# Moving the elementwise work of a two-layer hybrid network's fronts from GpSimd to VectorE

## The chip, the cores and the metric

The kernel runs on one core of a Trainium2 chip. What is measured is the time of one execution on the device, in microseconds (us). A core has five engines that work at the same time, each through its own queue and in the order of that queue: TensorE (PE in the rows; PEld is its weight load), VectorE (DVE), ScalarE (ACT), GpSimd (POOL) and SyncE (SP), which here only issues DMAs. Engines wait for one another by semaphores.

## The reference

Two layers of a diffusion backbone over 256 latent tokens and 256 context tokens, width 1024, float32. A layer is, cut to what matters:

```
h      = modulate(rmsnorm(x), shift, scale)
ua, ub, uatt, us5, ug = split(h @ w_in)
y      = rwkv7(ua), gla(ub), window_attention(uatt), s5(us5)     # 4 mixers, width 256
merged = sum over i of sigmoid(ug_i) * (y_i @ w_branch[i])       # 4 gates, width 1024
x      = x + mod * (merged @ w_out)
tokens = modulate(rmsnorm(x), ...)
x      = x + mod * hierarchical_moe(tokens)    # top group of 4, top 2 of its 8 experts
```

RWKV-7 and S5 scan the tokens in both directions, GLA works in chunks of 64 tokens, attention has a window of 128, a sink and the context as keys. In the last layer the context tokens are only an input of the mixers, so there merges and MoE have 256 columns and not 512.

## The kernel before

**Stages.** A layer is a *front* (projection, mixers, gates, output projection, router) and a *MoE*. In the profiled execution the front of layer 0 ends at about 890 us, its MoE at about 1440 us, the front of layer 1 at about 2130 us, and the MoE of layer 1 ends the program. In a front, the first stretch (0 to 200 us, and 1440 to 1660 us) holds the S5 tables, S5's four groups of channels in both directions and GLA; then come RWKV's projection and attention; then RWKV's "units" (330 to 600 us, and 1780 to 1990 us), small chains of 64x64 matmuls and DVE operations, between which the matmuls of gate merges are woven; then the last merges and the tail.

**Weights in two parts.** Front matmuls take float32 weights as a rounded part and a remainder. `gsplit` (L237) loads 128x1024 weights into `g`, lets ACT copy them into a rounded tile `h`, and takes the remainder `r = g - h`; both tiles are called `gs` in the rows. `proj` (L255) multiplies by `h` first, 16 matmuls, and by `r` last, 8 matmuls. Tile `r` has two places in most stretches and one in the units and merges of layer 0 (L1852), so a subtraction can start when PE has let go of the `r` before the last, or of the last. There are 53 such pairs in each front.

**Who does the elementwise work.** The helpers `act`, `tt`, `stt` and `mm` (L270 to L286) issue nearly everything, so most rows carry their lines; `tt` goes to DVE unless it is given another engine. Before, GpSimd has: the remainders; the token shift sums `us` of RWKV (L338); one of four key products `bk` of each RWKV unit (L493, the other three are on DVE); the end-of-chunk key product `ke` of GLA (L749) and half of the copies of its state, `sb` (L798); two of the six rope operations per token tile (L860, L863); of the S5 quarters one of each two products (`t<-fq,tb`, L1197, L1200, L1214); the remainder `hl` of half of the modulated activations (L1330); the sum of merges in `acc` (L1397); the second half of the residual `x` (L1410); and the split of every second token tile for the MoE (L1436). It also sets tiles to constants (memset), and in the MoE it adds expert results.

**Order.** The program is written as a list of operations; a scheduler then puts each engine's instructions in an order of its own by a plan, so that one engine's queue mixes instructions of several mixers. At run time no instruction passes another of its queue.

Of the kernel before, what the change touches and what calls it, by code (L numbers as in the profile page):

```python
# [175 lines left out]
class Net:  # L176
# [60 lines left out]
    def gsplit(self, src):  # L237

        w = self.gload(src)
        k, n = src.shape[1:]  # L240
        i = self.gi % 2
        self.gi += 1
        h, r = (p.tile([128, 1024], F32R, tag=t, name="gs")[:, 0:k * n].rearrange("p (k n) -> p k n", k=k)
                for p, t in (self.gp[i], self.gp[2 + i]))
        self.act(h, w, AF.Copy)
        self.tt(r, w, h.bitcast(F32), OP.subtract, self.nc.gpsimd)
        return h, r

    def mm3(self, out, a, b, start, stop):
# [44 lines left out]
    def rwkv_in(self, l, h, lo, pool, tp, between):  # L294
# [29 lines left out]
        for sec in (3, 1, 0, 2):  # L324
            for hf in range(2):
                a, n = (lo, nlo) if sec == 0 else (0, 512)
                ns = n // 256
                ps = self.pa()
                self.proj(ps[:, 0:n], io["w_in_rwkv"][l, 2 * sec + hf], h, a)
                between()  # L330
                ci = sec * 2 + hf
                u = tp.tile([128, 2, 258], F32, tag="upad", name="u")
                G.memset(u[:, :, 0:258:257], 0.0)
                psv = ps[:, 0:n].rearrange("p (s t) -> p s t", t=256)
                self.act(u[:, 0:ns, 1:257], psv, AF.Copy)
                s = tp.tile([128, 512], F32, tag="us", name="us")
                sv = s[:, 0:n].rearrange("p (s t) -> p s t", t=256)
                self.tt(sv, u[:, 0:ns, 0:256], u[:, 0:ns, 2:258], OP.add, G)  # L338
                dst = xa[:, hf, :] if sec == 3 else r[:, hf, :] if sec == 0 else kv[:, sec - 1, hf, :]
                self.act(dst, ps[:, 0:n], AF.Copy, scale=omu[:, ci:ci + 1])  # L340
                self.stt(dst, s[:, 0:n], hmu[:, ci:ci + 1], dst, OP.mult, OP.add)
# [68 lines left out]
    def rwkv_finish(self, l, hf, st, y, pool):  # L410

        prm = self.prm[l]
        r, k_, v, lo = st["r"], st["k"], st["v"], st["lo"]
        blk = self.cst[:, C_BLK:C_BLK + 128]
        nlo = 512 - lo
        ps = self.pc()
        self.mm(ps[:, 0:nlo], blk, y, True, True)
        yc = pool.tile([128, nlo], F32, tag="yc", name="yc")
        self.stt(yc, ps[:, 0:nlo], -1.0 / 64, y, OP.mult, OP.add)
        s2 = st["pool"].tile([128, 512], F32, tag="pi", name="s2")[:, 0:nlo]  # L420
        self.act(s2, yc, AF.Square)
        ps = self.pc()
        self.mm(ps[:, 0:nlo], blk, s2, True, True)
        self.rsq(s2, ps[:, 0:nlo], 1.0 / 64, 1)
        self.stt(yc, yc, prm[:, P_LNG + hf:P_LNG + hf + 1], s2, OP.mult, OP.mult)
        self.stt(s2, r[:, hf, :], prm[:, P_RK + hf:P_RK + hf + 1], k_[:, hf, lo:512], OP.mult, OP.mult)
        ps = self.pc()
        self.mm(ps[:, 0:nlo], blk, s2, True, True)
        self.tt(s2, ps[:, 0:nlo], v[:, hf, lo:512], OP.mult)
        self.tt(yc, yc, s2, OP.add, self.nc.gpsimd)  # L430
        ps = self.pc()
        self.mm(ps[:, 0:nlo], st["g2"][:, hf * 128:hf * 128 + 128], st["sg"], True, True)
        self.tt(y, ps[:, 0:nlo], yc, OP.mult)
# [30 lines left out]
    def rwkv_sub(self, hf, d, s, u, S0, st, na, y, pool):  # L464
# [16 lines left out]
        n = st["n"]  # L481
# [8 lines left out]
        for f in range(2):  # L490
            fv = fo[f][:, ts].rearrange("p (j t) -> p j t", t=64)
            self.tt(bk[E[f], :, f, :], ch(na[:, ts])[E[f]], fv[E[f]], OP.mult)
            self.tt(bk[E[1 - f], :, f, :], ch(k_[:, hf, ts])[E[1 - f]], fv[E[1 - f]], OP.mult, V if f else G)  # L493

        sm = st["p0"].tile([128, 4, 2, 192], F32, tag="sm", bufs=st["depth"], name="sm")
        for jp in range(2):
# [235 lines left out]
    def gla_dir(self, d, la, q, kx, v, mg, oT, lo, pool):  # L732
# [13 lines left out]
        ke = pool.tile([128, 512], F32, tag="ke", name="ke")  # L746
        self.tt(ke.rearrange("p (c t) -> p c t", t=64), tot.to_broadcast([128, 8, 64]), c3, OP.subtract)
        self.act(ke, ke, AF.Exp, scale=1.0 / 16)
        self.tt(ke, ke, kx, OP.mult, G)  # L749
        qd = pool.tile([128, 512], F32, tag="qd", name="qd")  # L750
        self.act(qd[:, lo:512], cum[:, lo:512], AF.Exp, scale=1.0 / 16)
        self.tt(qd[:, lo:512], qd[:, lo:512], q[:, lo:512], OP.mult)
# [40 lines left out]
        for hp in range(2):  # L793
            for e in range(2):
                h = 2 * hp + e
                r = slice(32 * h, 32 * h + 32)
                for n, c in runs:
                    (G if e else V).tensor_copy(sb[r, c, e, :], S[r, n - 1, :])  # L798
                ps = self.pb()
                for c in range(c0, 8):  # L800
                    b, t = c % 2, c // 2
                    self.mm(ps[64 * b:64 * b + 64, 64 * t:64 * t + 64], ki[r, 64 * c:64 * c + 64],
                            qd[r, 64 * c:64 * c + 64], True, True)
                for b in range(2):
                    rb = slice(64 * b, 64 * b + 64)
                    self.tt(sc[rb, e, t0:4, b, :], ps[rb, 64 * t0:256].rearrange("p (t n) -> p t n", n=64),
                            mg[rb, None, :].to_broadcast([64, 4 - t0, 64]), OP.mult)
# [20 lines left out]
    def attn(self, l, h, yT, lo, pool):  # L828
# [23 lines left out]
        for t in range(2, 4):  # L852
# [4 lines left out]
            o = rot.rearrange("p (h z n) -> p h z n", h=6, z=2)  # L857
            tm = tm.rearrange("p (z h n) -> p z h n", z=2, h=6)
            self.tt(o[:, :, 0, :], raw[:, :, 0, :], cs, OP.mult)
            self.tt(tm[:, 0], raw[:, :, 1, :], sn, OP.mult, G)  # L860
            self.tt(o[:, :, 0, :], o[:, :, 0, :], tm[:, 0], OP.subtract)
            self.tt(o[:, :, 1, :], raw[:, :, 0, :], sn, OP.mult)
            self.tt(tm[:, 1], raw[:, :, 1, :], cs, OP.mult, G)  # L863
            self.tt(o[:, :, 1, :], o[:, :, 1, :], tm[:, 1], OP.add)
            qk[t] = rot
        qT = pool.tile([128, 2, 512], F32, name="qT")
# [253 lines left out]
    def s5_quarter(self, d, gb, lo, pr, tb, ug, ys, kd, t2, dd, pool):  # L1120
# [73 lines left out]
        zq = pool.tile([128, 2, 4, 64], F32, tag="zq", name="zq")  # L1194
        C, S_ = tb[:, 0, g4], tb[:, 1, g4]
        self.tt(s1[:, 0], fq[:, 0], C, OP.mult)
        self.tt(s1[:, 1], fq[:, 1], S_, OP.mult, G)  # L1197
        self.tt(zq[:, 0], s1[:, 0], s1[:, 1], OP.add)
        self.tt(s1[:, 0], fq[:, 1], C, OP.mult)
        self.tt(s1[:, 1], fq[:, 0], S_, OP.mult, G)  # L1200
        self.tt(zq[:, 1], s1[:, 0], s1[:, 1], OP.subtract)
        rh = pool.tile([128, 4, 64], F32, tag="rh", name="rh")
        self.tt(rh, self.mres[:, 0:256].rearrange("p (g n) -> p g n", g=4),
# [7 lines left out]
        for z in range(2):  # L1211
            a, b = (fq[:, 0], fq[:, 1]) if z == 0 else (fq[:, 1], fq[:, 0])
            self.tt(s1[:, 0], a, C, OP.mult)
            self.tt(s1[:, 1], b, S_, OP.mult, G)  # L1214
            op = OP.subtract if z == 0 else OP.add
            if d == 0:
                self.tt(xi[:, z, :, 1:64], s1[:, 0, :, 0:63], s1[:, 1, :, 0:63], op)
# [106 lines left out]
    def modulate(self, k, mc, h, src, tmp):  # L1324

        for s in range(2):
            t = slice(256 * s, 256 * s + 256)
            self.tsc(tmp[:, t], src[:, t], mc[:, 0, s, k:k + 1], OP.mult, mc[:, 1, s, k:k + 1], OP.add)
        self.act(h[0][:, k, :], tmp, AF.Copy)
        self.tt(h[1][:, k, :], tmp, h[0][:, k, :].bitcast(F32), OP.subtract, None if k % 2 else self.nc.gpsimd)  # L1330

    def rows(self, l, pool):

# [36 lines left out]
    def merge(self, l, i, h, yT, acc, lo, first, pool, between, pairs=None):  # L1370
# [5 lines left out]
        for c in range(8):  # L1376
# [17 lines left out]
                self.stt(o, sg, 1.0, pb, OP.add, OP.mult)  # L1394
            else:
                self.stt(sg, sg, 1.0, pb, OP.add, OP.mult)
                self.tt(o, o, sg, OP.add, nc.gpsimd)  # L1397

    def project(self, t, w, acc, x, bs, lo, pool):

# [2 lines left out]
        for n in range(2):  # L1403
# [3 lines left out]
            tm = pool.tile([128, 512], F32, tag="pm", bufs=2, name="pm")  # L1407
            self.tt(tm, ps, bs[s][:, 512 * n:512 * n + 512], OP.mult)
            xo = x[t][:, 512 * n:512 * n + 512]
            self.tt(xo, xo, tm, OP.add, self.nc.gpsimd if n else None)  # L1410


    def norm2(self, t, x, rw, lo, h2p, wr, lg, pool):
# [19 lines left out]
            (V.tensor_copy if kb else nc.scalar.copy)(hT[:, 4 * kb:4 * kb + 4, :].rearrange("p k n -> p (k n)"), ps)  # L1433
        for k in range(8):
            self.mm(lg[:, 36 * tl:36 * tl + 36], hT[:, k, :], wr[:, k, :], k == 0, k == 7)
        self.split3([h2p[:, i, tl, :] for i in range(3)], h2, G if t % 2 else V)  # L1436

    def split3(self, o, r, eng):

# [467 lines left out]
```

## Time and profile before

| | |
|---|---|
| three runs | 2632.54, 2640.57, 2654.95 us (median 2640.57) |
| profiled execution | 2633.36 us, of which the span is 2631.5 us |
| mean granted TensorE clock | 0.939 |
| busy: PE, DVE, ACT, POOL | 2392.9, 1167.7, 665.1, 705.6 us |
| front 0, MoE 0, front 1, MoE 1 (about) | 890, 550, 690, 500 us |

Busy times are sums over the span. "Idle before" counts the time in which an engine had nothing to run, and is put down to the work whose end came last. PEclk is the granted clock of TensorE in a stretch, where 1 is the higher of its two levels (2.4 GHz) and 0.5 the lower (1.2 GHz). A row `gs<-g,gs` is an instruction that writes a tile `gs` from tiles `g` and `gs`.

### The profile page before, as it was taken

What the parts mean: (1) busy time and instruction counts of PE and PEld (TensorE: products, weight loads), DVE (VectorE), ACT (ScalarE), POOL (GpSimd) and SP (SyncE); (2) the same over time, 40 slices, a digit from 0 to 9 for tenths busy, and PEclk for the clock granted to TensorE, in tenths of its full rate; (3) what the DMA queues carried; (4) which work ended last, traced back from release to release, by engine and by line L of the source; (5) the groups of instructions that cost most, each with busy time, mean ns of one, the idle gap of its engine ahead of it and who ended that gap; (6) DMA issues with size and microseconds to landing.
All of it is one profiled execution on the core that took longest, in us unless ns stands there. A gap on an engine that the chain in (4) does not pass through costs nothing. (4 is left out here: it accounts for less than half of the span.)

```text
span 2631.5 us, 42668 instructions
## 1 busy us (share of the span) xinstructions
PE 2392.9 (91%) x17303; PEld 1445.7 (55%) x17303; DVE 1167.7 (44%) x3013; ACT 665.1 (25%) x1187; POOL 705.6 (27%) x603
## 2 busy tenths in 40 slices
PE   5889989999999899999999788998989899999997
PEld 4666756666764544444443665776777544333332
DVE  6685467573224533122222678558373432222212
ACT  3243433322211211111111324432323211111111
POOL 2233411213521232232233334422224211111111
PEclk8988989999999899999999798778889989999999
DMA  6332111214542698888886243312224579999994
GB/s 222 107 122 89 60 42 36 69 37 171 191 168 87 276 389 352 320 326 316 351 317 271 94 157 127 105 47 64 60 75 166 220 312 419 411 394 403 390 405 166
DMA packets 143693, 548.24 MB, mean 208 GB/s; under 512 B 35028, under 2 KB 66132, under 8 KB 93060
## 3 DMA queue, kind: packets, MB, share of 16 engines
q1 hardware_dynamic: 138224, 539.51, 54.0%
q10 hardware_dynamic: 5268, 5.94, 0.7%
q8 instruction: 140, 2.29, 0.4%
q14 instruction: 61, 0.50, 0.1%
HBM read 541.78 MB, written 3.60 MB: 207 GB/s over the span
## 5 line engine op out<-in xcount | busy, mean ns | idle before, releaser
L270 PE MATMUL pa<-hh,gs 128*128 128x512 f32 (+2 forms) x1440 | 436.6, 378 | 12.0 <-ACT sg L273 4.3
L276 POOL TENSOR_TENSOR gs<-g,gs 128x1024 fp32r<-128x1024 f32 (+1 forms) x106 | 258.6, 2443 | 581.9 <-PE pa L270 231.2
L276 POOL TENSOR_TENSOR ta<-ta,mb 128x512 f32<-128x512 f32 x93 | 127.8, 1381 | 835.5 <-ACT ta L273 835.5
L270 PEld LDWEIGHTS pa<-hh,gs 128*128 128x128 f32 (+1 forms) x1440 | 265.2, 198 | 74.5 <-issue 18.3
L270 PE MATMUL pd<-w,hT 128*64 128x512 f32 x1024 | 276.6, 599 | 13.1 <-ACT hT L273 12.4
L270 PE MATMUL pa<-hl,gs 128*128 128x512 f32 (+2 forms) x720 | 263.2, 377 | 0.0
L270 PE MATMUL pgate<-w,xT 128*64 128x512 f32 x1024 | 251.3, 596 | 0.0
L270 PE MATMUL pup<-w,xT 128*64 128x512 f32 x1024 | 249.2, 594 | 0.0
L270 PEld LDWEIGHTS <-h2p 128*128 128x128 bf16 x2304 | 135.2, 100 | 78.0 <-issue 72.6
L270 PE MATMUL pg<-oh,h2p 128*128 128x128 bf16 x2304 | 163.5, 223 | 5.9 <-DVE nv L1686 4.2
L273 ACT ACTIVATE gs<-g 128x1024 fp32r<-128x1024 f32 (+1 forms) x106 | 110.4, 1044 | 221.9 <-PE pa L270 139.6
L270 PEld LDWEIGHTS pd<-w,hT 128*64 128x64 f32 x1024 | 81.5, 136 | 146.7 <-issue 124.6
L270 PEld LDWEIGHTS pa<-hl,gs 128*128 128x128 f32 (+1 forms) x720 | 144.6, 201 | 28.4 <-issue 9.4
L270 PEld LDWEIGHTS pup<-w,xT 128*64 128x64 f32 x1024 | 78.3, 137 | 143.2 <-issue 139.3
L270 PEld LDWEIGHTS pgate<-w,xT 128*64 128x64 f32 x1024 | 74.7, 137 | 139.6 <-issue 129.5
L270 PE MATMUL py<-yp,oT 128*128 128x512 f32 x384 | 132.3, 438 | 11.2 <-ACT ta L273 5.1
L286 DVE SCALAR_TENSOR_TENSOR hd<-hd,pgate 128x512 f32<-128x512 f32 x32 | 22.0, 688 | 246.4 <-ACT hd L273 246.3
L276 POOL TENSOR_TENSOR x<-x,ta 128x512 f32<-128x512 f32 x93 | 121.6, 1314 | 4.9
L270 PE MATMUL pa<-gs,hh 128*128 128x256 f32 x480 | 112.9, 330 | 7.3 <-POOL gs L276 6.9
L276 DVE TENSOR_TENSOR hd<-hd,pup 128x512 f32<-128x512 f32 x32 | 22.0, 688 | 217.9 <-PE pup L270 217.9
L286 DVE SCALAR_TENSOR_TENSOR yp<-pd,ws,yp 128x512 fp32r<-128x512 f32 x64 | 47.8, 747 | 152.6 <-ACT yp L273 152.6
L273 ACT ACTIVATE yp<-pd,ws 128x512 fp32r<-128x512 f32 x64 | 44.1, 688 | 272.9 <-PE pd L270 272.9
(505 smaller groups left out, 3692.1 us busy)
## 6 DMA issues: line engine op xcount, KB each, us to landing
w<-in_w_g SPq DMA_DIRECT2D x128, 1024.0 KB, 7.8
w<-in_w_d SPq DMA_DIRECT2D x128, 1024.0 KB, 10.3
w<-in_w_u SPq DMA_DIRECT2D x128, 1024.0 KB, 8.5
g<-in_w_ada SPq DMA_DIRECT2D x96, 512.0 KB, 3.7
g<-in_w_in_gate SPq DMA_DIRECT2D x64, 512.0 KB, 3.7
g<-in_w_in_rwkv SPq DMA_DIRECT2D x16, 512.0 KB, 3.6
wb<-in_w_branch SPq DMA_DIRECT2D x64, 128.0 KB, 2.9
w<-in_w_out SPq DMA_DIRECT2D x8, 1024.0 KB, 8.0
```

The source lines that it names most:

```text
L270: self.nc.tensor.matmul(out, lhsT, rhs, start=start, stop=stop, skip_group_check=True)
L273: self.nc.scalar.activation(out, in_, f, **kw)
L276: (eng or self.nc.vector).tensor_tensor(out, a, b, op)
L286: self.nc.vector.scalar_tensor_tensor(out, a, s, b, op0=op0, op1=op1)
```

## The change

Every `tt` of the list above loses its engine argument, or is given DVE, so that DVE runs it; the copies of GLA's state that GpSimd made are made by ACT. What is left to GpSimd in a front are memsets and copies of constants at the start. The MoE (`pair`) is as before. No tile, pool or loop is changed. The edits are all of one kind; the core of the diff:

```diff
@@ gsplit
         self.act(h, w, AF.Copy)
-        self.tt(r, w, h.bitcast(F32), OP.subtract, self.nc.gpsimd)
+        self.tt(r, w, h.bitcast(F32), OP.subtract)
@@ rwkv_in
-                self.tt(sv, u[:, 0:ns, 0:256], u[:, 0:ns, 2:258], OP.add, G)
+                self.tt(sv, u[:, 0:ns, 0:256], u[:, 0:ns, 2:258], OP.add)
@@ rwkv_finish
-        self.tt(yc, yc, s2, OP.add, self.nc.gpsimd)
+        self.tt(yc, yc, s2, OP.add)
@@ rwkv_sub
             self.tt(bk[E[f], :, f, :], ch(na[:, ts])[E[f]], fv[E[f]], OP.mult)
-            self.tt(bk[E[1 - f], :, f, :], ch(k_[:, hf, ts])[E[1 - f]], fv[E[1 - f]], OP.mult, V if f else G)
+            self.tt(bk[E[1 - f], :, f, :], ch(k_[:, hf, ts])[E[1 - f]], fv[E[1 - f]], OP.mult)
@@ gla_dir
-        self.tt(ke, ke, kx, OP.mult, G)
+        self.tt(ke, ke, kx, OP.mult)
...
-                    (G if e else V).tensor_copy(sb[r, c, e, :], S[r, n - 1, :])
+                    (nc.scalar.copy if e else V.tensor_copy)(sb[r, c, e, :], S[r, n - 1, :])
@@ attn (the same for tm[:, 1])
-            self.tt(tm[:, 0], raw[:, :, 1, :], sn, OP.mult, G)
+            self.tt(tm[:, 0], raw[:, :, 1, :], sn, OP.mult)
@@ s5_quarter (three lines of this kind)
-        self.tt(s1[:, 1], fq[:, 1], S_, OP.mult, G)
+        self.tt(s1[:, 1], fq[:, 1], S_, OP.mult)
@@ modulate
-        self.tt(h[1][:, k, :], tmp, h[0][:, k, :].bitcast(F32), OP.subtract, None if k % 2 else self.nc.gpsimd)
+        self.tt(h[1][:, k, :], tmp, h[0][:, k, :].bitcast(F32), OP.subtract)
@@ merge
-                self.tt(o, o, sg, OP.add, nc.gpsimd)
+                self.tt(o, o, sg, OP.add)
@@ project
-            self.tt(xo, xo, tm, OP.add, self.nc.gpsimd if n else None)
+            self.tt(xo, xo, tm, OP.add)
@@ norm2
-        self.split3([h2p[:, i, tl, :] for i in range(3)], h2, G if t % 2 else V)
+        self.split3([h2p[:, i, tl, :] for i in range(3)], h2, V)
```

The scheduler gives every engine a new order. On DVE, in the first stretch of layer 0, the power tables of S5 are made in a chain of small operations (`t` is a pair of products, `w` their sum or difference, `tb` the table). Before:

```order
L276 TENSOR_TENSOR t_474<-w_1077 128x8 x2
L276 TENSOR_TENSOR w_1090<-t_474 128x8
L276 TENSOR_TENSOR t_474<-w_1077 128x8 x2
L276 TENSOR_TENSOR w_1090<-t_474 128x8
L276 TENSOR_TENSOR t_474<-tb,w_1090 128x8x16 x2
```

With the change:

```order
L276 TENSOR_TENSOR t_474<-w_1077 128x8 x2
L276 TENSOR_TENSOR gs<-g,gs 128x1024
L276 TENSOR_TENSOR w_1090<-t_474 128x8
L286 SCALAR_TENSOR_TENSOR rg<-th__1933,pa 128x512
L276 TENSOR_TENSOR t_474<-w_1077 128x8 x2
L276 TENSOR_TENSOR w_1090<-t_474 128x8
L276 TENSOR_TENSOR t_474<-tb,w_1090 128x8x16 x2
```

A remainder now stands inside the chain, ahead of a 128x8 difference.

On DVE, in the RWKV units of layer 1, the key products `bk` of one unit stand between steps of a triangular inverse (`ti`, `tm`) of another. Before (the product `bk<-kv,sw` is on GpSimd):

```order
L276 TENSOR_TENSOR tm<-lt,ti 128x4x9
L276 TENSOR_TENSOR bk<-na,sw 64x4x64
L276 TENSOR_TENSOR ti<-ti,tm 128x4x9
L276 TENSOR_TENSOR ti<-ti,tm 128x4x14
L276 TENSOR_TENSOR tm<-lt,ti 128x4x8
L276 TENSOR_TENSOR bk<-na,ic 64x4x64
L276 TENSOR_TENSOR ti<-ti,tm 128x4x8
L276 TENSOR_TENSOR tm<-lt,ti 128x4x13
L276 TENSOR_TENSOR tm<-lt,ti 128x4x7
L276 TENSOR_TENSOR bk<-kv,ic 64x4x64
```

With the change:

```order
L276 TENSOR_TENSOR gs<-g,gs 128x1024
L276 TENSOR_TENSOR tm<-lt,ti 128x4x15
L276 TENSOR_TENSOR ar_15166<-na,pp 128x4x64
L276 TENSOR_TENSOR ti<-ti,tm 128x4x15
...
L276 TENSOR_TENSOR bk<-na,sw 64x4x64
L276 TENSOR_TENSOR tm<-lt,ti 128x4x12
L276 TENSOR_TENSOR bk<-kv,sw 64x4x64
L276 TENSOR_TENSOR ti<-ti,tm 128x4x12
L276 TENSOR_TENSOR bk<-na,ic 64x4x64
L276 TENSOR_TENSOR tm<-lt,ti 128x4x11
L276 TENSOR_TENSOR bk<-kv,ic 64x4x64
```

All four products are in DVE's queue now, and a remainder stands twelve instructions ahead of the first.

On DVE, in GLA of layer 1, where `ke` is made. Before (`ke<-e` is the exponent; the product `ke<-ke,kx` is on GpSimd):

```order
L276 TENSOR_TENSOR ke<-e 128x512
L276 TENSOR_TENSOR t_12472<-pw,bb 128x512 x2
L276 TENSOR_TENSOR qd<-qd,q 128x256
L276 TENSOR_TENSOR ba<-t_12472 128x512
L276 TENSOR_TENSOR ki<-ki,kx 128x256
```

With the change:

```order
L276 TENSOR_TENSOR ke<-e 128x512
L276 TENSOR_TENSOR t_12472<-u_12545 128x8 x2
L276 TENSOR_TENSOR qd<-qd,q 128x256
L276 TENSOR_TENSOR w_13432<-t_12472 128x8
L276 TENSOR_TENSOR ki<-ki,kx 128x256
L276 TENSOR_TENSOR t_12472<-u_12545 128x8 x2
L740 SCALAR_TENSOR_TENSOR e<-mres,e 128x512
L276 TENSOR_TENSOR w_13432<-t_12472 128x8
L276 TENSOR_TENSOR ke<-ke,kx 128x512
```

The product follows the exponent after seven other instructions, and S5's work around it is of an earlier step (`w` tables where `ba` stood).

## Rows read from the trace of the kernel before

**Rows 1.** Busy time of each engine, from the page; share, instructions.

```profile
PE 2392.9 (91%) x17303; PEld 1445.7 (55%) x17303; DVE 1167.7 (44%) x3013; ACT 665.1 (25%) x1187; POOL 705.6 (27%) x603
```

**Rows 2.** Windows of the fronts: length, busy PE PEld DVE ACT POOL, PEclk, DMA, GB/s.

```profile
0.00:200.00 200.00, 150.60 (x1421) 120.57 (x1423) 142.78 (x418) 63.68 (x114) 54.06 (x70) 0.88 0.44 149
200.00:890.00 690.00, 644.94 (x4879) 443.06 (x4877) 334.14 (x934) 208.61 (x381) 187.16 (x149) 0.95 0.29 99
1440.00:1660.00 220.00, 179.24 (x1608) 135.98 (x1603) 161.04 (x442) 70.86 (x128) 76.69 (x87) 0.86 0.36 118
1660.00:2130.00 470.00, 420.30 (x3624) 322.87 (x3625) 249.29 (x737) 152.58 (x287) 147.08 (x116) 0.87 0.32 108
```

**Rows 3.** Waits of PE: who, for whom; us in total, times, longest.

```profile
PE psc L270 <- DVE bk L276: 18.8, 6, 6.1
PE pc L760 <- POOL ke L276: 12.5, 3, 6.7
PE pb L270 <- DVE ba L276: 11.8, 6, 4.3
PE pa L270 <- POOL gs L276: 10.6, 9, 2.0
```

**Rows 4.** Timeline in S5's tables: start, us, operation, count, idle before.

```profile
138.66 0.17 DVE L276 TENSOR_TENSOR w<-t 128x8 f32<-128x8 f32 x1
138.87 0.25 DVE L276 TENSOR_TENSOR t<-w 128x8 f32<-128x8 f32 x2
...
141.20 4.74 POOL L276 TENSOR_TENSOR gs<-g,gs 128x1024 fp32r<-128x1024 f32 x2 [16.07 <-ACT gs L273]
141.36 2.26 DVE L276 TENSOR_TENSOR w<-t 128x8 f32<-128x8 f32 x1
143.66 2.40 DVE L276 TENSOR_TENSOR t<-w 128x8 f32<-128x8 f32 x2
...
150.95 0.44 PE L1150 MATMUL pb<-cst,ba 128*128 128x128 f32 x2 [4.17 <-DVE ba L276]
```

**Rows 5.** Timeline in the RWKV units of layer 1.

```profile
1912.24 2.79 POOL L276 TENSOR_TENSOR gs<-g,gs 128x1024 fp32r<-128x1024 f32 x1
1912.76 2.34 DVE L276 TENSOR_TENSOR tm<-lt,ti 128x44 f32<-128x44 f32 x1
1915.02 0.41 DVE L276 TENSOR_TENSOR bk<-na,sw 64x256 f32<-64x256 f32 x1
1915.11 1.02 POOL L276 TENSOR_TENSOR bk<-kv,sw 64x256 f32<-64x256 f32 x1
1917.42 2.34 PE L270 MATMUL psc<-ar,bk 64*128 64x192 f32 x8 [6.10 <-DVE bk L276]
```

**Rows 6.** Windows behind that stall, and after it.

```profile
1916.50:1933.40 16.90, 15.45 (x58) 12.12 (x59) 13.20 (x59) 3.27 (x9) 3.75 (x3) 0.50 0.30 90
1933.60:1950.00 16.40, 16.07 (x268) 13.59 (x267) 13.36 (x62) 4.90 (x10) 3.09 (x2) 1.00 0.24 65
```

**Rows 7.** Groups of POOL: count, busy, mean ns, idle before and its enders.

```profile
L276 POOL TENSOR_TENSOR gs<-g,gs 128x1024 fp32r<-128x1024 f32 x104 | 257.2, 2476 | 550.2 <-PE pa L270 199.5 <-ACT gs L273 161.9 <-issue 72.1
```

**Rows 8.** Groups of DVE: count, busy, mean ns, idle before and its enders.

```profile
L276 DVE TENSOR_TENSOR h<-h,h2p 128x1024 f32<-128x1024 f32 x3 | 3.6, 1216 | 0.0
L276 DVE TENSOR_TENSOR x<-x,pm 128x512 f32<-128x512 f32 x6 | 4.2, 694 | 0.2
L276 DVE TENSOR_TENSOR yy<-psw,dd 128x256 f32<-128x256 f32 x16 | 6.8, 423 | 10.2 <-PE psw L270 8.5 <-ACT ic L273 1.6
L276 DVE TENSOR_TENSOR bl<-wb,bh 128x256 fp32r<-128x256 f32 x40 | 33.4, 838 | 10.6 <-ACT bh L273 10.4
L276 DVE TENSOR_TENSOR zq<-t 128x252 f32<-128x252 f32 x8 | 9.8, 1220 | 2.1 <-POOL t L276 2.1
```

**Rows 9.** Group of ACT with small copies.

```profile
L273 ACT ACTIVATE cd<-s5cr 64x64 f32<-64x64 f32 x16 | 4.0, 252 | 6.9 <-PE pb L270 6.7
```

**Rows 10.** POOL's remainders by window: length, busy (count), PEclk, DMA, GB/s.

```profile
0.00:200.00 200.00, 27.08 (x12) 0.88 0.44 149
330.00:600.00 270.00, 33.73 (x14) 0.94 0.17 47
1440.00:1660.00 220.00, 36.12 (x14) 0.86 0.36 118
1780.00:1990.00 210.00, 37.56 (x16) 0.87 0.21 60
```

More of the change, by code (lines that the diff above doesn't have):

```diff
@@ L859, in attn @@
             self.tt(o[:, :, 0, :], raw[:, :, 0, :], cs, OP.mult)
-            self.tt(tm[:, 0], raw[:, :, 1, :], sn, OP.mult, G)
+            self.tt(tm[:, 0], raw[:, :, 1, :], sn, OP.mult)
             self.tt(o[:, :, 0, :], o[:, :, 0, :], tm[:, 0], OP.subtract)
             self.tt(o[:, :, 1, :], raw[:, :, 0, :], sn, OP.mult)
-            self.tt(tm[:, 1], raw[:, :, 1, :], cs, OP.mult, G)
+            self.tt(tm[:, 1], raw[:, :, 1, :], cs, OP.mult)
             self.tt(o[:, :, 1, :], o[:, :, 1, :], tm[:, 1], OP.add)
@@ L1196, in s5_quarter @@
         self.tt(s1[:, 0], fq[:, 0], C, OP.mult)
-        self.tt(s1[:, 1], fq[:, 1], S_, OP.mult, G)
+        self.tt(s1[:, 1], fq[:, 1], S_, OP.mult)
         self.tt(zq[:, 0], s1[:, 0], s1[:, 1], OP.add)
         self.tt(s1[:, 0], fq[:, 1], C, OP.mult)
-        self.tt(s1[:, 1], fq[:, 0], S_, OP.mult, G)
+        self.tt(s1[:, 1], fq[:, 0], S_, OP.mult)
         self.tt(zq[:, 1], s1[:, 0], s1[:, 1], OP.subtract)
@@ L1213, in s5_quarter @@
             self.tt(s1[:, 0], a, C, OP.mult)
-            self.tt(s1[:, 1], b, S_, OP.mult, G)
+            self.tt(s1[:, 1], b, S_, OP.mult)
             op = OP.subtract if z == 0 else OP.add
```

## The prediction

> **What bounds the kernel now.** I read the busy times first, then the windows of the fronts, then PE's waits, then the timeline ahead of the longest of those waits, and last the groups of POOL and DVE. TensorE sets the time: it is busy 2392.9 of 2631.5 us, DVE 44%, POOL 27% [rows 1]. The reader should see that a change of elementwise work can gain or lose only what PE's idle time and its clock allow. The MoEs keep their code, so only the four windows of the fronts count [rows 2]. There PE is idle 49.4 + 45.1 + 40.8 + 49.7 = 185 us, and it is granted 0.88, 0.95, 0.86 and 0.87 of its clock. With levels of 1 and 0.5, twice the missing share times the length is the time at the lower level: 48 + 69 + 62 + 122 = 301 us. So the fronts hold two things to be won: stalls, and the slow stretches.
>
> DVE is not idle everywhere in them: it is busy 71% and 73% of the two S5 and GLA windows, and 48% and 53% of the others [rows 2].
>
> Part of that busy time is not work. A 128x8 difference takes 0.17 us and a pair of products 0.25 us; two microseconds later, under a remainder on POOL, the same two take 2.26 and 2.40 us [rows 4]. DVE lost 4.2 us there, and the next rows show PE waiting 4.17 us for the `ba` at the end of that chain. In the RWKV units it is the same in part: a small product takes 2.34 us under POOL's remainder, while PE waits 6.10 us for `bk` [rows 5]; that remainder also held back the key product behind it on POOL, from 1912.24 to 1915.11. Over the whole trace 40 `bl` of 128x256 take 838 ns where `yy`, of the same size but with one input from PSUM, takes 423; `zq` of 128x252 takes 1220 [rows 8]. POOL pays too: 2476 ns for a remainder that DVE does at 1216 ns [rows 7, 8]. So in these rows the two engines hold each other up.
>
> **The change part by part.** It moves to DVE, by count of the edited lines: 110 operations of 128x1024 (104 remainders and 6 of the token split), about 58 of 512 columns and about 86 of 256 or fewer. At 1.22, 0.69 and 0.42 us [rows 8] that is 134 + 40 + 36 = 210 us of new DVE work. It removes the time in which DVE was held. Two groups show it directly: 40 x (838 - 423) = 17 us and 8 x (1220 - 423) = 6 us [rows 8]. At most it is POOL's whole busy time in the four windows, 465 us [rows 2], and at least those 23. I take 150: half of POOL's time is likely its own waiting (2476 ns against 1216), and DVE is busy some six tenths of the rest, 465 x 0.5 x 0.6 = 140. So DVE's load grows by about 60 us in fronts of 1580 us: it is not the sum of DVE's work that decides, but where in its queue it stands.
>
> *At nothing* I cost the sums of merges, shifts, rope, `hl`, the residual and `yc`, some 55 us of DVE: they lie between 200 and 890 us and 1660 and 2130 us, beside matmuls that need none of them for microseconds, on a DVE busy half of the time. If that cover is gone, the next merge's `acc` waits, not PE. No DMA is moved; the place of `g` comes free 1.3 us sooner, and the DMA engines, 29 to 44% busy [rows 2], take that.
>
> *Stalls ended by POOL* [rows 3]: 12.5 us for `ke` and 10.6 us for `gs`, 23.1 in all. Both get a 1.22- or 0.69-us operation on DVE where a 2.48- or 1.39-us one stood on a queue behind remainders. In the new order the `ke` product stands seven instructions behind its exponent, most of them small. I take 15 us of the 23; the bounds are 23 (all) and, if DVE's queue makes them as late as POOL's did, 0.
>
> *Stalls ended by DVE* [rows 3]: 18.8 for `bk` and 11.8 for `ba`, 30.6 in all. In [rows 4] the loss under POOL, 4.2, covers the whole wait; in [rows 5] it is 2.1 of 6.1. I take 60% as held, 18 us. Against it stands a remainder of 1.22 us that now sits in the chain itself, as the order shows for the S5 table and, twelve instructions ahead, for the key products; a chain that was held for 2 to 4 us by one or two remainders now does one or two of them. I keep 10 us; bounds 30 and -10.
>
> *The clock.* Behind the stall of [rows 5] PE runs 16.9 us at 0.50, busy 91% of it, and then is back at 1.00 [rows 6]. So a stall costs itself and a slow stretch. Of the 301 us at the lower level PE is busy about 90%, so half of that, 135 us, would go if it never fell. I take the share in proportion to idle time: 25 of 185 us is 14%, and 14% of 135 is 18 us. Bounds: 0, if the stalls that remain are enough to bring the clock down, and 38 if all 53.7 us of [rows 3] went.
>
> *What is added to the path.* 44 state copies go to ACT at about 0.25 us [rows 9], 11 us beside ACT's 32% load in the two S5 windows; GLA's chain of states waits for them, I count 4 us, bounds 0 and 11. In each tail, the split of the last tile now stands between DVE operations of the router: two of 1.22 less 0.6 for the residual sum that becomes faster (0.69 on DVE), 0.6 us at each end, about 1. New waits in DVE's queue, for a remainder whose place PE has not let go: 5. Together about 10 us.
>
> The sum against the profiled execution's 2633.4: 15 + 10 + 18 - 10 = 33 us, or **2600 us**. That execution lies 0.3% under the median of the three runs; I leave the number, the range takes in those 7 us.
>
> **A rule that speaks against it.** The Trainium skill, Perfetto Trace Analysis, section "Optimizing Scalar/DVE Operations", says that work may be offloaded from a saturated DVE, to ScalarE or even to GpSimd, and adds that offloading between GpSimd and DVE may not help since they share a port. Its first half would have this change undone in the S5 windows, and the null or slower case below would follow; its second half, which [rows 4] bear out with 2.26 us for 0.17, is why I don't give it more. No run here shows DVE above 73%, so I don't call it saturated.
>
> **The rivals.**
>
> *All of it goes.* If every one of the stalls in [rows 3] was made by the two engines holding each other, and DVE absorbs the new work in its gaps, 53.7 + 38 = 92 us go: 2541 us. For it: [rows 4], where the numbers agree to 0.1 us. Against: [rows 5], where two thirds of the wait stay unexplained. Chance 0.13.
>
> *DVE takes as much as it was held.* In the DVE-heavy windows new work and lost holding balance: 56 remainders stand there [rows 10], 68 us of DVE time at 1.22, with S5's products and `ke` beside them. If the holding that went was about the same, chains end when they did, and only `gs` and `ke` gain some: about -5, 2628 us. For it: the S5 order with a remainder ahead of a 128x8 difference. Chance 0.23.
>
> *The queue blocks.* Slower by this mechanism: POOL spent 199.5 us waiting for PE to let go of a remainder's tile and 161.9 us for ACT's copy ahead of a remainder [rows 7]. On POOL little stood behind them; on DVE, which takes nothing out of order, the whole of S5's and RWKV's chains does. If the scheduler's plan puts remainders too early by its own clock, each waits in front of the chain. It decides from some 0.6 us of mean wait on the 56 remainders [rows 10] on, which makes 34 us and eats the gain; at 1.2 us each, 67 us less the 33, it gives 2668 us. For it: TensorE runs slower than any plan could know at clock 0.5. Against: the remainders are wanted eight or more matmuls later, so a planner has slack to put them late. Chance 0.14.
>
> That the change does less than it says can be left out: the order shows every moved operation on DVE.
>
> **How the numbers follow.** The forecast case, 15 to 60 us gained (2573 to 2618), has 0.50. The range of 2548 to 2647 holds it, the null case, and a third of each of the two outer ones. For the signs I count from the median of before, where 1% is 26 us, about what a measurement of this kernel can tell from no change: under 2614 lie most of the forecast (0.43) and all of the first rival (0.13), 0.56; between, the null case and the upper end of the forecast, 0.28; above 2667, the blocked queue and a bad order, 0.16.
>
> **What would show it.** Right: 128x8 operations on DVE at 0.17 us or less everywhere in the fronts, `bl` at 0.42 to 0.45 us, remainders on DVE at 1.2 us; the waits of PE for `ke`, `ba` and `bk` down by half; clocks of the fronts up by a few hundredths; DVE busy some 1230 us, POOL some 300. Wrong: `gs` on DVE with long idle time put down to PE's `pa` or ACT's `gs`, and PE's waits for `bk`, `ba`, `zq` longer than they were; or PE's idle time in the fronts unchanged near 185 us, with the clock where it was. The share of held time in DVE's 1167.7 us is the number I know least: if it is near its low bound of 23 us, DVE's load in the two S5 windows rises from 304 to about 350 of 420 us (26 remainders and 32 products more), and the forecast falls with it.

## The result and the profile after

The changed kernel takes 2528.04 us (median of 4 runs, 2508.66 to 2535.16) against 2637.53 us before: a ratio of 0.958 (95% interval 0.954 to 0.962). On another chip it was run again and stood at 0.952 (0.945 to 0.959). Below, "over the changed kernel" means the difference of a run's ratio to the middle of these two, 0.955, times 2640 us; a ratio is uncertain by some 0.005, so such a difference by some 12 us. The gain is 110 us on the first chip and 128 on the other; 119 is their mean and the figure used below. The forecast was 33, and its range ended at 2548.

The profiled execution (2508.66 us, span 2506.9) is the fastest of the first four: its granted clock is 0.967, that of the other three 0.958 to 0.960. The page's busy times, to be held against [rows 1]:

```profile
PE 2329.0 (93%) x17303; PEld 1397.5 (56%) x17303; DVE 1202.6 (48%) x3267; ACT 670.5 (27%) x1229; POOL 278.0 (11%) x305
```

DVE was given 210 us of work, by the prediction's count, and is busy only 35 us longer. DVE's instructions overlap one another in the trace, though, so that a count of durations has to be held against the sum of durations and not against busy time. The durations of all its instructions add up to 1297.7 us before and 1362.1 after, 64 more. So 146 us of DVE's time before was not work.

The windows of the two fronts, cut where the first gate matmul of a MoE starts or the last one ends (columns as in [rows 2]). Before:

```profile
0.00:879.30 879.30, 784.84 (x6244) 560.01 (x6244) 474.56 (x1345) 271.31 (x492) 241.22 (x218) 0.93 0.32 109
1436.60:2124.60 688.00, 597.54 (x5221) 458.13 (x5217) 409.88 (x1174) 223.59 (x416) 225.02 (x205) 0.87 0.34 111
```

After:

```profile
0.00:819.30 819.30, 753.63 (x6242) 538.63 (x6242) 499.64 (x1474) 272.65 (x517) 15.02 (x61) 0.97 0.35 117
1376.90:2000.40 623.50, 564.79 (x5219) 431.19 (x5215) 419.72 (x1299) 227.53 (x433) 23.91 (x64) 0.92 0.38 123
```

All of the gain is here: 60.0 + 64.5 = 124.5 us; the MoE between is 557.3 and 557.6 us long. It has two halves. PE's idle time in the fronts falls from 94.5 + 90.5 = 185 to 65.7 + 58.7 = 124 us, 61 less. PE's busy time, for the same matmuls, falls from 1382.4 to 1318.4 us, 64 less: that is the clock. (A second profiled execution of the changed kernel, of 2518.50 us, has 129 us of idle time and 1323.5 us of PE work in the fronts; the clock's part of the gain is 59 us there.) By the prediction's reckoning (twice the missing share times the length), the time at the lower level falls from 301 to some 150 us.

PE's waits that answer to [rows 3]:

```profile
PE psc L270 <- DVE bk L276: 8.1, 5, 2.2
PE pc L760 <- DVE ke L276: 3.1, 1, 3.1
PE pa L270 <- DVE gs L276: 2.4, 4, 1.0
```

The wait for `ba` of S5's small products, 11.8 us before, has no row left. Of 53.7 us, 13.6 stay. The 4.17 us that PE waits in [rows 4] are of another row, which [rows 3] lack; before, and then after:

```profile
PE pb L1150 <- DVE ba L276: 6.8, 4, 4.2
...
PE pb L1150 <- DVE ba L276: 2.0, 2, 1.3
```

DVE's groups that answer to [rows 8], and the remainders that came to it:

```profile
L276 DVE TENSOR_TENSOR gs<-g,gs 128x1024 fp32r<-128x1024 f32 x104 | 127.3, 1226 | 74.0 <-PE pa L270 54.7 <-ACT gs L273 14.9 <-PE po L270 2.4
L276 DVE TENSOR_TENSOR bl<-wb,bh 128x256 fp32r<-128x256 f32 x40 | 16.6, 420 | 12.6 <-ACT bh L273 12.6
L276 DVE TENSOR_TENSOR zq<-t 128x252 f32<-128x252 f32 x8 | 3.3, 416 | 0.1
```

`bl` falls from 838 to 420 ns and `zq` from 1220 to 416, the length that `yy` had all along [rows 8]. The remainders wait on DVE for PE 54.7 us and for ACT's copy 14.9 us, as the blocked-queue rival said, but that is a fifth of what they waited on GpSimd [rows 7], and PE's wait for `gs` did not grow with it.

### The profile page after: what moved, and what is told of

Its sections match the earlier page's. It is cut to its first block, busy times and chain, and to the rows that moved or that the text cites. A ratio compares the mean times of both kernels' runs of the same rounds, so it can differ in the third digit from the quotient of the medians.

```text
span 2506.9 us, 42482 instructions
## 1 busy us (share of the span) xinstructions
PE 2329.0 (93%) x17303; PEld 1397.5 (56%) x17303; DVE 1202.6 (48%) x3267; ACT 670.5 (27%) x1229; POOL 278.0 (11%) x305
## 5 line engine op out<-in xcount | busy, mean ns | idle before, releaser
L270 PE MATMUL pa<-hh,gs 128*128 128x512 f32 (+2 forms) x1440 | 421.2, 366 | 10.2 <-ACT sg L273 6.1
L270 PEld LDWEIGHTS pa<-hh,gs 128*128 128x128 f32 (+1 forms) x1440 | 252.4, 188 | 69.8 <-issue 15.3
L270 PE MATMUL pa<-hl,gs 128*128 128x512 f32 (+2 forms) x720 | 252.8, 363 | 0.0
L276 DVE TENSOR_TENSOR gs<-g,gs 128x1024 fp32r<-128x1024 f32 (+1 forms) x106 | 128.1, 1211 | 83.2 <-PE pa L270 56.7
L270 PEld LDWEIGHTS pa<-hl,gs 128*128 128x128 f32 (+1 forms) x720 | 137.1, 190 | 27.3 <-issue 9.1
L276 DVE TENSOR_TENSOR tm<-py,mb 128x512 f32<-128x512 f32 x99 | 66.7, 687 | 95.7 <-PE py L270 95.7
```

The costliest lines, as they stand in the source:

```text
L270: self.nc.tensor.matmul(out, lhsT, rhs, start=start, stop=stop, skip_group_check=True)
L276: (eng or self.nc.vector).tensor_tensor(out, a, b, op)
```

## The experiments

Four theories were tested. A: what costs is that DVE is held while GpSimd reads SBUF. B: GpSimd's results came late. C: the new order is better by chance. Rival from the prediction: DVE's added load eats what it wins.

**Useless reads put back on GpSimd**, behind each split (`d` is a tile of its own that nobody reads):

```diff
         self.tt(r, w, h.bitcast(F32), OP.subtract)
+        self.tt(d, h.bitcast(F32), h.bitcast(F32), OP.subtract, self.nc.gpsimd)
```

> The changed kernel, to which GpSimd adds one useless subtraction of two SBUF inputs (the rounded tile minus itself, 128x1024) behind each of the 106 weight splits; nobody reads its result, and DVE keeps its new order and all of its new work. If the two engines hold each other up when both read SBUF (theory A), DVE's operations stretch again as they did before, DVE's busy time grows by some 100 us (106 of them at about 2.5 us, 260 of the former 434 us of GpSimd reads, of a hold of 175 us), and the time rises by 60 to 130 us over the changed kernel, to 2590 to 2660 us. If the gain came because GpSimd's results came late (theory B), or because the scheduler's new order is better (theory C), the time stays within 15 us of the changed kernel's 2528.

Measured: 2618.42 us, ratio 0.993 (0.990 to 0.996), 100 us over the changed kernel. The page's busy times, then GpSimd's new group, PE's longest wait of those above, and a piece of the timeline in S5's tables:

```profile
PE 2387.3 (91%) x17303; PEld 1435.3 (55%) x17303; DVE 1320.0 (50%) x3267; ACT 670.9 (26%) x1229; POOL 504.6 (19%) x411
...
L279 POOL TENSOR_TENSOR dm<-gs 128x1024 bf16<-128x1024 f32 x104 | 225.5, 2168 | 824.7 <-ACT gs L276 824.1
...
PE psc L273 <- DVE bk L279: 19.9, 5, 5.5
...
145.49 0.28 DVE L279 TENSOR_TENSOR tb<-t 128x128 f32<-128x128 f32 x1
...
146.15 1.91 POOL L279 TENSOR_TENSOR dm<-gs 128x1024 bf16<-128x1024 f32 x1 [7.07 <-ACT gs L276]
146.34 1.86 DVE L279 TENSOR_TENSOR tb<-t 128x128 f32<-128x128 f32 x1
```

The same sum takes 0.28 us alone and 1.86 under the read, and ends with it. Nothing waits for GpSimd in this kernel, yet DVE is busy 117 us longer with the same 3267 instructions, PE's wait for `bk` is back at 19.9 us, and 84% of the gain is gone. DVE's instructions stand in the order of the changed kernel in all but one place, so C cannot be the main cause, and B cannot either.

**The control, which only writes**:

```diff
         self.tt(r, w, h.bitcast(F32), OP.subtract)
+        self.nc.gpsimd.tensor_copy(d[:, 0, 0:1], h[:, 0, 0:1].bitcast(F32))
+        for _ in range(2):
+            self.nc.gpsimd.memset(d, 0.0)
```

> The control of the run above: in the same places GpSimd does one 128x1 copy and two memsets of 128x1024 into the same unused tile, so it is nearly as busy and waits for the same tiles, but all it does is write. Theory A: within 15 us of the changed kernel (2528), since memsets read nothing. If it rises like the run with reads, it isn't reading that holds DVE but any work on GpSimd, or the waits that the additions brought. Theories B and C: the same as the run with reads.

Measured: 2531.95 us, 0.961 (0.956 to 0.966), 15 us over, at the edge of what can be told. Busy times and the group of memsets:

```profile
PE 2346.2 (93%) x17303; PEld 1406.2 (56%) x17303; DVE 1207.8 (48%) x3267; ACT 670.5 (27%) x1229; POOL 523.8 (21%) x623
...
L251 POOL MEMSET dm<- 128x1024 bf16 x208 | 198.3, 953 | 11.9
```

GpSimd is busier than in the run before, and DVE 5 us longer busy, not 117. Reading holds DVE; work on GpSimd does not. The Trainium skill, SBUF — State Buffer, section "Who interferes with whom", says the same: a DVE instruction with two SBUF inputs contends with a GpSimd instruction that reads SBUF, not with one that only writes it. Of the 15 us, 5 lie in the MoE of layer 0, which is 562 us long and not 558; it is so in every run that has the unused tile, whichever engine writes it, so the figures "over the changed kernel" of those runs are some 5 us too high as a price of what they add.

**The remainders alone, and all but the remainders.** The first is the kernel before with only the edit in `gsplit`; the second is the changed kernel with that one edit undone:

```diff
-        self.tt(r, w, h.bitcast(F32), OP.subtract)
+        self.tt(r, w, h.bitcast(F32), OP.subtract, self.nc.gpsimd)
```

> The kernel before with one edit of the change: the 106 remainders go to DVE, all else stays on GpSimd. Theory A: GpSimd's reads in the fronts fall from 434 to about 175 us, so 60% of the gain of 110: about 2570 us. Theory B: the late products of the chains (ke, bk, S5's) are still on GpSimd but no longer behind remainders, so half or more of the gain, 2560 to 2580; it can't be told from A here but from the next run. Theory C: anything.

> The changed kernel with the remainders given back to GpSimd; all other operations stay on DVE. Theory A: the long reads of GpSimd are still there, 259 of 434 us, against a DVE with more to do: at most 40% of the gain, 2590 us or more, with DVE operations held for 2 us and longer. Theory B: the chains have nothing on GpSimd any more, so most of the gain is there, 2545 us or less; only PE's waits for remainders stay (10.6 us).

Measured: 2534.30 us, 0.963 (0.957 to 0.969), and 2607.34 us, 0.988 (0.983 to 0.993). One edited line brings 98 of the 119 us; the eleven other edits by themselves 31. Three groups of DVE in the second run:

```profile
L276 DVE TENSOR_TENSOR bl<-wb,bh 128x256 fp32r<-128x256 f32 x40 | 28.0, 706 | 14.3 <-ACT bh L273 14.1
L276 DVE TENSOR_TENSOR us<-u 128x512 f32<-128x512 f32 x14 | 19.8, 1416 | 8.6 <-ACT u L273 8.4
L276 DVE TENSOR_TENSOR bk<-na,sw 64x256 f32<-64x256 f32 x16 | 13.0, 813 | 0.1
```

What had come to DVE (`us`, 0.69 us alone) is now held there itself. The first run came out better than expected of A (2570). Its DVE was given 128 us of work and its durations add up to 31 us more, so 97 of the 146 us of holding went: two thirds, where the gain is four fifths. The rest of that gain has no cause shown here.

**The same work on DVE instead.**

```diff
         self.tt(r, w, h.bitcast(F32), OP.subtract)
+        self.tt(d, h.bitcast(F32), h.bitcast(F32), OP.subtract)
```

> The changed kernel with the same useless 128x1024 subtraction behind each of the 106 weight splits, but on DVE: 129 us more of DVE work, and nothing on GpSimd. If DVE's load were what the change had to pay with (my rival in which DVE takes as much as it was held), 129 us more should cost 40 us or more, since before the change DVE lost some 147 us in the fronts by being held, and that cost 110. If what costs is being held at a place that the plan of the order knows nothing of (theory A, sharper), planned work of the same size finds gaps: 2528 to 2550 us.

Measured: 2568.81 us, 0.970 (0.966 to 0.975), 40 us over. Its group:

```profile
L279 DVE TENSOR_TENSOR dm<-gs 128x1024 bf16<-128x1024 f32 x104 | 127.3, 1224 | 27.5 <-ACT gs L276 26.9
```

By theory A I had expected at most 22 us over, so the result falls at the start of the rival's branch, with its 40. DVE's load does cost, 40 for 127, 0.31 us for each us; but held time costs more than twice as much (100 for 117). The rival had a real price and too small a size. The scheduler gave DVE another order here than in the changed kernel, so the 40 us are the price of the work and of that order together.

**Is it the length of one hold?** The useless reads in 4 to 8 pieces, and as a copy with one input:

```diff
+        for j in range(k):
+            self.tt(d[:, j], h[:, j].bitcast(F32), h[:, j].bitcast(F32), OP.subtract, self.nc.gpsimd)
```

```diff
+        self.nc.gpsimd.tensor_copy(d, h.bitcast(F32))
```

> The run with useless GpSimd reads (2618 us), each subtraction in pieces of 128x128 or 128x256 (4 to 8 for a split) with the same tiles, the same bytes and the same order on the other engines. If the sum of GpSimd's reading is what counts, the time stays at 2600 to 2630. If the length of one hold counts (a 0.17-us DVE operation then waits for 0.3 to 0.7 us at most, and not 2.3), most of the loss goes: 2535 to 2575. The kernel with only the remainders moved, 49 us of DVE still held in the fronts by shorter GpSimd operations and yet 2534 us, speaks for the latter.

> The same place and tiles, but GpSimd does one copy of 128x1024 (one SBUF input instead of two). If a read through one input holds DVE as well, its loss goes by the copy's duration against 2.4 us: with 1 to 1.5 us each, 2550 to 2590 us. If only two-input operations of GpSimd hold DVE, 2528 to 2540, as with memsets.

Measured: 2575.04 us, 0.973 (0.970 to 0.977), 49 over, and 2565.17 us, 0.970 (0.965 to 0.975), 39 over. GpSimd's groups and busy times of the pieces, then of the copies:

```profile
PE 2371.6 (92%) x17303; PEld 1423.3 (55%) x17303; DVE 1267.7 (49%) x3267; ACT 670.6 (26%) x1229; POOL 695.4 (27%) x1089
...
L280 POOL TENSOR_TENSOR dm<-gs 128x128 bf16<-128x128 f32 x704 | 358.8, 545 | 571.6 <-ACT gs L277 571.6
```

```profile
PE 2368.3 (92%) x17303; PEld 1421.2 (55%) x17303; DVE 1248.1 (49%) x3267; ACT 670.7 (26%) x1229; POOL 412.1 (16%) x411
...
L249 POOL CAST dm<-gs 128x1024 bf16<-128x1024 f32 x104 | 134.0, 1288 | 853.5 <-ACT gs L276 853.4
```

The loss of the pieces halves, as the second reading said, but so does the time that DVE is held. Over the changed kernel's DVE:

| run | DVE held longer, us | time over, us | ratio of the two |
|---|---|---|---|
| whole reads | 117 | 100 | 0.85 |
| pieces | 65 | 49 | 0.75 |
| one input | 46 | 39 | 0.85 |
| writes only | 5 | 15 | - |

With 12 us of uncertainty in each time, the three ratios can't be told apart: it is the sum of held time that counts, some 0.8 us for each us, and no effect of the length of one hold is seen. A read through one input holds DVE too.

**Filling one stall of PE.** In the tails of the changed kernel PE waits 5.2 us for the last normalized tile:

```diff
+        if t == 3:
+            ps = self.pa("fill")
+            for i in range(11):
+                self.mm(ps, self.ident, xs[:, 512 * (i % 2):512 * (i % 2) + 512], True, True)
```

> The changed kernel with 11 matmuls of 128x512 that nobody reads, in both tails, at the place where PE waits some 5.2 us for the last normalized tile (in the trace the clock is at its lower level for 23.9 us behind it, with 13.6 and 12.5 us of PE work). If each stall costs a second time by the clock, the two slow stretches go and with them up to half of that work, 13 us: 2512 to 2525 us. If the router's chain on DVE sets the time there anyway, nothing changes, or the fill delays the transposes by up to 1 us each: 2526 to 2532.

Measured: 2530.47 us, 0.955 (0.950 to 0.960), nothing. Windows of the tail of layer 0, of the changed kernel and then with the fill (PEclk is the third column from the end):

```profile
784.00:791.40 7.40, 6.12 (x18) 2.92 (x16) 1.85 (x6) 1.15 (x2) 0.00 (x0) 1.00 0.78 293
791.50:815.40 23.90, 13.62 (x80) 11.46 (x81) 15.92 (x67) 5.79 (x11) 0.00 (x0) 0.50 0.52 215
```

```profile
787.00:799.00 12.00, 12.00 (x35) 5.68 (x35) 5.87 (x18) 1.15 (x2) 0.00 (x0) 1.00 0.09 13
799.00:827.00 28.00, 27.96 (x104) 15.45 (x102) 13.17 (x33) 6.91 (x10) 0.00 (x0) 1.00 0.84 332
827.40:841.10 13.70, 5.92 (x66) 5.82 (x67) 8.92 (x45) 2.35 (x8) 0.00 (x0) 0.50 0.01 1
```

The clock stays at 1.00 over the filled place and falls at the next wait, for 13.7 us and not 23.9. The slow stretch got shorter, and the time did not: here it bought nothing. That the router's chain on DVE sets the time there is the likely reason; no run shows it by itself.

**GpSimd's queue full, but only of writes.** The kernel with the remainders alone moved, and two memsets of the remainder's tile ahead of each subtraction:

```diff
+        for _ in range(2):
+            self.nc.gpsimd.memset(r.bitcast(F32), 0.0)
         self.tt(r, w, h.bitcast(F32), OP.subtract)
```

> The kernel before with the remainders on DVE (2534 us), and in their place on GpSimd two memsets of the remainder's tile ahead of each subtraction: GpSimd's queue is as full of things that wait for PE to let go of a tile as it was before the change, with the products ke, bk, us and S5's behind them, but these things only write. It separates lateness from holding. The runs so far give 0.8 us for each us that DVE is held in the fronts and 0.3 us for each us of planned DVE work; from before (147 held, 0) to the changed kernel (5 held, 210 us of work) that makes -114 + 63 = -51, and 60 of the 114 stay over. If the products' lateness on GpSimd is the rest (theory B as a second cause), this run is 40 to 60 us over the kernel with only the remainders moved: 2575 to 2595. If holding is all, 2530 to 2545.

Measured: 2571.73 us, 0.973 (0.969 to 0.978), 27 us over its base in ratio (0.963), between the two expectations. It is not the clean test it was meant to be. Busy times and PE's waits:

```profile
PE 2368.5 (92%) x17303; PEld 1423.6 (55%) x17303; DVE 1198.3 (47%) x3119; ACT 663.5 (26%) x1188; POOL 655.9 (26%) x709
...
PE pa L272 <- DVE gs L278: 10.4, 6, 3.2
PE psc L272 <- DVE bk L278: 9.9, 6, 2.6
PE pc L762 <- POOL ke L278: 1.8, 2, 1.2
```

DVE is busy 17 us longer than in its base (1181.4) with the same instructions, so the products' reads moved to worse places, and at 0.8 that makes 14. PE's wait for `gs` is 10.4 us against 5.0 in the base, likely because of the memsets before it, that for `bk` 9.9 against 6.6; `ke` is not late (1.8 against 8.0). What is left, some 13 us, is no larger than what can be told.

**Four operations, `ke` alone on DVE**, in the kernel before:

```diff
-        self.tt(ke, ke, kx, OP.mult, G)
+        self.tt(ke, ke, kx, OP.mult)
```

> The kernel before with four operations of the change: GLA's product ke goes to DVE. GpSimd's reading falls by 5.5 us only, so by holding alone it gains 5 us at most. If the 12.5 us that PE waited for ke are lateness in GpSimd's queue, behind the remainders, and each us of a stall costs about as much again by the clock, 15 to 25 us are gained: a ratio of 0.990 to 0.994. If DVE, held by the remainders as before, makes ke as late as GpSimd did, nothing is gained: 0.998 to 1.002.

Measured: 2622.74 us, 0.993 (0.991 to 0.996): 18 us for four instructions. PE's wait for `ke` falls from 12.5 us [rows 3] to

```profile
PE pc L760 <- DVE ke L276: 4.7, 1, 4.7
```

So PE waits 7.8 us less for `ke`. But that is not how the time was won. The windows of the fronts (cut as above):

```profile
0.00:880.20 880.20, 786.99 (x6244) 562.92 (x6244) 470.55 (x1347) 271.34 (x492) 237.48 (x216) 0.92 0.33 109
1437.70:2113.30 675.60, 584.51 (x5223) 450.42 (x5217) 410.70 (x1176) 222.47 (x416) 220.16 (x203) 0.89 0.35 113
```

All of PE's idle time in them is 184 us, against 185 before; other waits grew (that for `sc` from 4.0 to 7.0 us). PE's busy time fell by 11 us, as much as the two profiled spans differ: what was won there is the clock. The four instructions are worth 18 us, with an interval from 11 to 25, and by holding 5 at most; so holding is not all of the gain. That lateness on GpSimd is the second cause fits, but the way from it to the time is not shown.

**Three more edits of the changed kernel**: 108 small copies of the units and GLA from DVE to ACT (`V.tensor_copy` to `nc.scalar.copy`); the MoEs' sums from GpSimd to DVE; GLA's state copies from ACT back to GpSimd:

```diff
-                if n and pooled[t]:
+                if False:
```

```diff
-                    (nc.scalar.copy if e else V.tensor_copy)(sb[r, c, e, :], S[r, n - 1, :])
+                    (G if e else V).tensor_copy(sb[r, c, e, :], S[r, n - 1, :])
```

> The changed kernel with 108 small DVE copies of the units and of GLA's states (25 us) given to ACT. By 0.3 us for each us of DVE work, 8 us are to be won: 2515 to 2525 us. If ACT's own queue makes the copies late, it stays or rises by up to 10 us.

> The changed kernel with the last GpSimd readers gone as well: in both MoEs the sums of expert results (127 + 123 us on GpSimd) go to DVE, straight from PSUM, and ACT's copies of them fall away. DVE is held there some 10 us now, but the MoEs move weights with 85 to 91% of the DMA engines' time and their lengths (557 and 506 us) did not change with the fronts: within 10 us of the changed kernel. If holding costs 0.8 us for each us everywhere, 8 us less, and 130 us more of DVE work would cost 39.

> The changed kernel with the 44 state copies of GLA back on GpSimd, which reads SBUF there for 15 us in all, and not on ACT. By 0.8 us for each us that DVE is held, up to 12 us are lost if each copy holds DVE for all of its 0.35 us; with one copy in three meeting DVE, 4 us: 0.953 to 0.960 of before. It bounds the part of the prediction in which ACT's copies were to cost 4 us.

> The changed kernel itself once more, on the chip of these runs, so that they are compared with it there: 0.953 to 0.963 of the time of the kernel before.

Measured: copies on ACT 2540.49 us, 0.962 (0.957 to 0.966), slower by some 18 us where 8 were to be won or at most 10 lost, although DVE has less to do; MoEs on DVE 2517.55 us, 0.954 (0.950 to 0.959), the same; state copies on GpSimd 2527.43 us, 0.956 (0.952 to 0.960), the same; the changed kernel again 2511.77 us, 0.952. In the run with copies on ACT, PE's idle time in the fronts is 134 us, against 124 and 129 in the two profiled executions of the changed kernel, and its busy time is longer by 22 and 17; which copies do it was not tried. The MoEs' group on DVE, in the changed kernel and then with their sums moved:

```profile
L276 DVE TENSOR_TENSOR x<-x,tm 128x512 f32<-128x512 f32 x99 | 77.4, 796 | 1.0
...
L276 DVE TENSOR_TENSOR x<-x,tm 128x512 f32<-128x512 f32 x192 | 126.0, 684 | 0.8
```

It falls from 796 ns, held by GpSimd, to 684. In its trace the two MoEs are 11 us shorter (548.7 and 504.2 us against 557.6 and 506.5), and the fronts are 15 and 6 us longer than in the two profiled executions of the changed kernel, so that in the whole time nothing shows beyond the uncertainty. No version is shown to beat the changed kernel.

## Why the prediction was wrong

The direction and the mechanism were right, and the range was missed because the sizes were too small. By its own steps, in the profiled executions:

- **The clock failed most.** "I take the share in proportion to idle time: 25 of 185 us is 14%, and 14% of 135 is 18 us." PE's busy time in the fronts fell by 64 us. The profiled execution is the fastest of its four, and the others differ from it by their clock; 20 us of the 64 go with it at the median, and what is left is still more than twice the 18. The step from idle time to clock does not hold: a stall's slow stretch is not proportional to the stall. [Rows 6] show 6.1 us of waiting and 16.9 us at 0.50; elsewhere in the kernel before, a wait of 1.28 us has as long a stretch behind it (timeline of PE, then the window):

```profile
355.32 0.50 PE L270 MATMUL pa<-hh,gs 128*128 128x512 f32 x1 [1.28 <-ACT gs L273]
```

```profile
356.60:373.50 16.90, 16.73 (x36) 10.59 (x36) 6.53 (x13) 4.10 (x9) 1.46 (x2) 0.50 0.25 73
```

  PE is busy 99% of that window, so half of it is lost. In the changed kernel PE waits as long at the same matmul, and nothing follows:

```profile
321.31 0.49 PE L270 MATMUL pa<-hh,gs 128*128 128x512 f32 x1 [1.28 <-ACT gs L273]
```

```profile
321.00:338.00 17.00, 16.15 (x63) 11.15 (x64) 11.22 (x38) 6.58 (x14) 0.00 (x0) 1.00 0.35 103
```

  In the whole record of the clock there are 32 stretches at the lower level with 321 us before, and 14 with 168 us after (17 with 182 in the second profiled execution). Of the 32, 25 begin within 8 us behind a wait of 0.4 us or more; of the 55 waits of 1 us or more, 17 have no such stretch behind or around them. So the stretches that went account for the term afterwards (half of 153 us, with PE busy nine tenths of it, is 69), but which of them a change takes away can't be read off the waits, and what brings the clock down at one wait and not at another stays open.
- **Small waits were left out: 20 us.** The sum dealt with the four waits of [rows 3]. They gave 40 us; PE's idle time in the fronts fell by 61. The rest are smaller waits, most of them on DVE: that for `ba` at L1150 (6.8 us before, 2.0 after), that of `mps` for `mods` (7.7 and 1.4), that of `pst` for `ti` (2.9 and 0.2). Not all fell: PE's wait for the DMA of `g` rose from 26.2 to 31.8 us.
- **Stalls ended by DVE**: 10 us taken, of 18 thought to be held; `bk` and `ba` gave 10.7 + 11.8 = 22.5. The remainder inside the chain did not give back half of it. Of the two cases that the 60% was taken from, that of [rows 4] is not in these 30.6 us.
- **Stalls ended by POOL**: 15 us taken, 23.1 - 5.5 = 17.6 measured. Right.
- **What is added to the path**: 10 us taken; putting the state copies back on GpSimd changed nothing that can be told. In the tails PE's wait for `hb` rose from 7.1 to 9.4 us and that for `h` fell from 13.0 to 10.3. About 0, within some 10 us.
- **Held time**: 150 us taken, 146 measured. Right in size, and by luck: "half of POOL's time is likely its own waiting" is wrong. The median of GpSimd's 106 remainders is 2392 ns, and of the 22 during which DVE is busy for less than a fifth, 19 take 2.34 to 2.41 us; in [rows 4] two take 4.74 us while DVE stands. It is DVE that waits. The other factor, six tenths, was too large by about as much (146 of 465 us is 0.31). The sentence on it, "it is not the sum of DVE's work that decides", was half wrong if the useless work is a measure: both sums have a price.

Together: 46 + 20 + 12 + 3 + 10 = 91 us short, against 124.5 - 33, in the profiled executions; at the median the first term is some 20 less.

The runs' own sum stands apart from that one, and it does not close. Holding, 146 us at 0.8, is 117 us, the whole of the gain. If DVE's new work cost 0.31 as the useless work did, 210 us would take back 65, and as much would have to come from lateness and from the new order; for that, `ke` shows 18. The two runs with parts of the change say the same:

| run | holding gone, us | new work, us | 0.8 of the one less 0.31 of the other | 0.8 of the one alone | measured gain |
|---|---|---|---|---|---|
| remainders alone | 97 | 128 | 38 | 78 | 98 |
| all but the remainders | 24 | 82 | -6 | 19 | 31 |
| the whole change | 146 | 210 | 52 | 117 | 119 |

The sums without a price for the moved work are nearer in all three. Either the moved work found cheaper places than the useless work did, or lateness and order paid for it; no run separates these. What is shown is the price of holding, by the useless reads and their control.

Of the rivals, the one that all of the stalls go (2541 us, chance 0.13) was nearest in number, but not all of them went (13.6 of 53.7 us stay), and it was short by the same clock term. The rival in which DVE takes as much as it was held put all 56 remainders of [rows 10] into the DVE-heavy windows; by those rows 26 stand in the two that are busy to 71 and 73%, the others in the units. The blocked queue did not come: the order put the remainders late enough that DVE waited for their inputs 74.0 us in all, beside other work.

## What to carry to other kernels

When an instruction takes ten times its usual time on DVE, look at what GpSimd reads in that moment: the held time is the sum of DVE's durations minus counts times clean durations, and here each us of it cost some 0.8 us, against 0.31 for useless work that stood in DVE's own order. So work that DVE does in half of GpSimd's time may belong on DVE even where DVE is the busier of the two, and one useless read on GpSimd, with a memset as its control, tells on the chip whether that is so. Look for the slow stretch behind a stall of TensorE in the granted clock before pricing the stall, and give that term a wide range: here a wait of 1.28 us had 17 us of it behind it in one kernel and none in the other.

## What was not expected of the hardware

- A GpSimd copy with one SBUF input (1288 ns each) holds two-input DVE operations as well, 46 us in all; a memset of the same size (953 ns) does not.
- Span times mean granted clock is nearly the same for all runs of a kernel: 2631.5 x 0.939 = 2471 before, and 2424 and 2423 in two runs after (2506.9 x 0.967, 2529.3 x 0.958). The spread between runs of one kernel, here 1%, is the clock's, and a single profiled execution shows one draw of it.
- Small copies of 0.2 to 0.3 us that moved from DVE to an ACT engine busy 27% of the time made the kernel slower by some 18 us; why is open.
